# A two-layer decoder trunk on one core: each 128x128 weight block as three 256-column products instead of a 512-column and a 256-column one

## The chip, the cores and the metric

The kernel runs on one core of one Trainium2 chip. The metric is device time in microseconds (us) of one execution; lower is better. The engines are called as the profile calls them: PE (TensorE, the matrix unit; PEld are its weight loads), DVE (VectorE), ACT (ScalarE), POOL (GpSimd) and SP (SyncE, which issues the weight transfers).

## The reference, cut to what matters

```python
h = x                                   # (1, 256, 2048) f32
for i in range(2):
    hn = rmsnorm(h, norm_mix_pre[i])
    mix = ssd_mixer(hn, ...) if i == 0 else fox_mixer(hn, ...)   # Mamba-2 SSD / forgetting attention
    h = h + rmsnorm(mix, norm_mix_post[i])
    g = rmsnorm(h, norm_ffn_pre[i])
    ff = (silu(g @ w_gate) * (g @ w_up)) @ w_down                # 2048 -> 5632 -> 2048
    h = h + rmsnorm(ff, norm_ffn_post[i])
    pe = rmsnorm(p[i] @ ple_w_proj[i], ple_norm[i])
    h = h + sigmoid(h @ ple_w_gate[i]) * pe
```

Everything is float32, and there are 256 tokens. Nearly all arithmetic is in the products with weight matrices: `ssd_w_in` (2048 x 10304), `ssd_w_out` (4096 x 2048), `fox_w_in` (2048 x 6160), `fox_w_out` (2048 x 2048), and for each layer gate, up, down, the small projection and its gate.

## The kernel before, in words

All activations lie transposed, channels on the 128 partitions and the 256 tokens along the free axis. Each operand of the `float32r` products is split in two: a high part `wh` and a remainder `wl` of the weights, and a high and a low half of each activation tile. One block is one 128x128 weight block times one activation tile, and it needs three terms: wh by high, wh by low, wl by high.

**Activation tiles.** `halves()` makes a tile of 576 columns and returns a view of two rows of 256 columns, the high half at column 0 and the low half at column 308 (`LOW_X`). `x[:, 0, :]` is the high half, `x[:, 1, :]` the low one. The tiles are called `x`, `xq`, `xb` or `a` by the pool that they come from.

**Weights.** The list `stages` holds, in order, all pieces of weights, each of up to 1024 columns (1 to 4 row blocks of 128). `emit_stage` issues for one piece the transfer (L191, on SP's queue, into one of six `raw` buffers), the cast to `wh` (L204, on ACT) and the remainder `wl = raw - wh` (L209, on DVE); there are four buffers each of `wh` and `wl`. There are 1020 such pieces.

**Units.** `unit(rhs, evac, ...)` takes the pieces of one matrix with 4 (sometimes 2, 5 or 6) output tiles. It takes one PSUM bank of 512 columns for each output tile (`acc`, six banks in rotation), and for each piece issues the products of each output tile and row block. There are three forms:
- `tok` (L260 to L262): tokens on the partitions, used for the V matrix of the attention layer, three products of 412 or 416 columns.
- `sep` (L266 to L268): three products of 256 columns, all into the first half of the bank. Only the last unit of each output matrix uses it (`sep=last` and the like).
- otherwise (L271 and L274): one product of 512 columns with `wh`, whose two halves go into the two halves of the bank, and one product of 256 columns with `wl`, added to the first half. All other units use it.

After the last piece, `evac(t, acc)` reads each output tile. In the 512-column form the bank's two halves have to be added: `gather` (L299 to L301) copies the second half to `tb` with ACT (L300) and adds it to the first half with DVE (L301) into the wanted tile. What follows is one more DVE multiplication or addition in many callers: by `rwide2` for the gates (`silu_a`, L614) and the z tiles (L1139, L1074), by the gate for the up matrix (L664), by `rwide` ahead of the convolution (L916), by `rq` or `rwide` for q and k (L1359, L1366), or added to `m` for the second half of the down matrix (L680). In `out_units`, in the first half of the down matrix, for `gz` and in the first gate unit of each layer the gathered tile is stored as it is.

**Order.** The instruction order on each engine is made by a scheduler that simulates a timeline, within constraints: `after(...)` and `tc.issue_after` tie an instruction behind another on its engine, `bg` is a list of small background tasks, one of which is issued after each piece, and `low`, `turn`, `turn_a`, `low_a` and `lag` keep the last cast and remainder, and what has to stand ahead of the next ones. `took` hands `gather`'s two instructions to `unit`, which in units of six tiles puts them ahead of the next cast and remainder.

Of the kernel before, what the change touches and what calls it, by code (L numbers as in the profile page):

```python
# [14 lines left out]
P = 128  # L15
# [48 lines left out]
def tile_trunk(ctx, tc, a, out):  # L64
# [159 lines left out]
    def unit(rhs, evac, tok=False, pre=None, pops=1, late=(), merge=1, look=LOOK, sep=False):  # L224
# [10 lines left out]
        while k0 < K:  # L235
# [12 lines left out]
            with after(p0):  # L248
                p = None
                for t in range(nt):  # L250
                    with after(p if ordered else None):
                        for wh, wl, kc, kb in held:
                            for c in range(kc):
                                k = kb + c
                                x = rhs(k)
                                st, sp = k == 0, k == K - 1
                                if tok:
                                    xh = x[:, 0, t * P:(t + 1) * P]
                                    o = accs[t][:, :n]
                                    PE.matmul(o, lhsT=xh, rhs=wh[:, c, :], start=st, stop=False)  # L260
                                    PE.matmul(o, lhsT=xh, rhs=wl[:, c, :], start=False, stop=False)  # L261
                                    last = PE.matmul(o, lhsT=x[:, 1, t * P:(t + 1) * P], rhs=wh[:, c, :],  # L262
                                              start=False, stop=sp)
                                elif sep:
                                    o, w = accs[t][:, :T], wh[:, c, t * P:(t + 1) * P]
                                    PE.matmul(o, lhsT=w, rhs=x[:, 0, :], start=st, stop=False)  # L266
                                    PE.matmul(o, lhsT=w, rhs=x[:, 1, :], start=False, stop=False)  # L267
                                    last = PE.matmul(o, lhsT=wl[:, c, t * P:(t + 1) * P], rhs=x[:, 0, :],  # L268
                                              start=False, stop=sp)
                                else:  # L270
                                    PE.matmul(accs[t].rearrange("p (a n) -> p a n", a=2),  # L271
                                              lhsT=wh[:, c, t * P:(t + 1) * P], rhs=x,
                                              start=st, stop=False)
                                    last = PE.matmul(accs[t][:, :T], lhsT=wl[:, c, t * P:(t + 1) * P],  # L274
                                              rhs=x[:, 0, :], start=False, stop=sp)
                    p = last
# [21 lines left out]
    def gather(acc, o, np_=P):  # L298
        tb = tmp("tb")  # L299
        i = A.copy(out=tb[:np_], in_=acc[:np_, T:2 * T])  # L300
        took[0] = (i, V.tensor_tensor(out=o, in0=acc[:np_, :T], in1=tb[:np_], op=add))  # L301
# [281 lines left out]
    def out_units(sizes, rhs, m_of, pre=None):  # L583
        c0 = 0
        for u, n in enumerate(sizes):
            last = u == len(sizes) - 1

            def e(t, acc, c0=c0, last=last):
# [5 lines left out]
                else:  # L594
                    gather(acc, m[c])
                    sumsq(ssb, m[c], c == 0)
            unit(rhs, e, pre=pre if u == 0 else None, merge=TAIL_STAGES if last else 1,
                 sep=last)
            c0 += n

    def tail(i, mpx, m, pp, mk_next):
# [3 lines left out]
        with ExitStack() as st:  # L605
# [7 lines left out]
            def silu_a(sg):  # L613
                last_v[0] = V.tensor_tensor(out=sg, in0=sg, in1=rwide2, op=mult)  # L614
                th = tmp("th")
                mark[0] = A.activation(th, sg, AF.Tanh)
                return th
# [5 lines left out]
            def ev_g(t, acc):  # L623
                sg = new_sg()
                gather(acc, sg)
                sgs.append(sg)
                if not first[0]:
                    silu_b(sg, silu_a(sg))
# [15 lines left out]
            for half in range(2):  # L644
                acts = [halves(ap_, tag="a", name=nm("a")) for _ in range(HALF)]
                c0 = 0
                for n in (GU if half == 0 else GU[::-1]):
# [8 lines left out]
                    def ev_u(t, acc, c0=c0, acts=acts, begun=begun):  # L656
# [6 lines left out]
                        gather(acc, up)  # L663
                        V.tensor_tensor(out=up, in0=up, in1=sgs[t], op=mult)  # L664
# [4 lines left out]
                for u in range(4):  # L669
                    def e2(t, acc, u=u, half=half):  # L670
# [6 lines left out]
                        else:  # L677
                            t2 = tmp("g0")
                            gather(acc, t2)
                            V.tensor_tensor(out=m[c], in0=m[c], in1=t2, op=add)  # L680
                            sumsq(ssb, m[c], c == 0)
                    unit(lambda k, acts=acts: acts[k], e2,
                         merge=TAIL_STAGES if half == 1 and u == 3 else 1,
                         sep=half == 1 and u == 3)
# [110 lines left out]
        for u, (n, todo) in enumerate(zip(OUT0, (pops0, pops1, pops2, pops3))):  # L795
            last = u == len(OUT0) - 1
            up = None
            if u == 0:
# [6 lines left out]
                 merge=TAIL_STAGES if last else 1, sep=last)  # L805
# [22 lines left out]
    with ExitStack() as ys:  # L828
        yp = pool(ys, "yp", side="right")
        y = [yp.tile([P, T], F32, name=f"y{c}") for c in range(32)]  # L830
        with ExitStack() as st:
# [240 lines left out]
            def z_a(t):  # L1072
                z = later[t][0]
                last_v[0] = V.tensor_tensor(out=z, in0=z, in1=rwide2, op=mult)  # L1074
                zt[t] = tmp("th")
                lag[1].append(A.activation(zt[t], z, AF.Tanh))
# [39 lines left out]
            def z_unit(g, pops):  # L1116
                S = {}

                def ev_z(t, acc):
# [3 lines left out]
                    if t == 0:  # L1123
                        S["ss"] = ssp
                        if g == 0:
                            gated(0, z00)
# [7 lines left out]
                    gather(acc, z)  # L1134
                    gated(t, z)

                def gated(t, z):
                    yc = y[4 * g + t]
                    V.tensor_tensor(out=z, in0=z, in1=rwide2, op=mult)  # L1139
# [29 lines left out]
        for t in range(4):  # L1169
            acc, yc, ss = later[t]  # L1170
            z = zp.tile([P, T], F32, name=f"z7_{t}")
            gather(acc, z)
            later[t] = (z, yc, ss)
        turn_a[0] = took[0][0]
# [177 lines left out]
    for u in range(4):  # L1352
# [3 lines left out]
        def ev_q(t, acc, q=q):  # L1356
            g0 = tmp("g0")
            gather(acc, g0)
            V.tensor_tensor(out=q[t], in0=g0, in1=rq, op=mult)  # L1359
# [3 lines left out]
        def ev_k(t, acc, kk=kk):  # L1363
            g0 = tmp("g0")
            gather(acc, g0)
            V.tensor_tensor(out=kk[t], in0=g0, in1=rwide, op=mult)  # L1366
# [92 lines left out]
```

## Time and profile before

| | |
|---|---|
| time, median of 3 runs | 2738.63 us (2738.59 to 2739.45) |
| time of the profiled execution | 2740.92 us |
| its span in the profile | 2739.1 us |
| PE busy | 2730.2 us (100%), 16342 products |
| PEld busy | 2419.8 us (88%) |
| DVE busy | 1905.3 us (70%) |
| ACT busy | 1481.6 us (54%) |
| HBM read | 514.58 MB, 189 GB/s over the span |

A row of the groups reads: line of the program, engine, operation, output<-inputs, shape, count, busy time, mean duration of one, idle time before them and what ended it. Products overlap in PE's pipeline, so the duration of one is longer than the distance from its start to the next start; the pace of PE is read from the starts, in the rows in order of time or in the first and last start of a group.

### The profile page before, as it was taken

To read this page: it belongs to the slowest core of one execution; us is meant where nothing else is said; L and a number is where in the kernel's file an instruction comes from. 1 tells how busy PE (TensorE), PEld (TensorE's weight loads), DVE (VectorE), ACT (ScalarE), POOL (GpSimd) and SP (SyncE) were. 2 spreads that over 40 slices of the span, in tenths; PEclk is the share of its full clock that TensorE was granted. 3 is DMA by queue.
4 is the path that set the end of the run, shared out by engine and by line. 5 is a ranking of instruction groups with operands and counts; after the bars stand their busy time and mean duration, and the time that the engine had idled before them with its cause. 6 is when DMAs were issued, how large, how long until landed. Compare 5 with 4: busy or idle time off the path is not lost.

```text
span 2739.1 us, 43140 instructions
## 1 busy us (share of the span) xinstructions
PE 2730.2 (100%) x16342; PEld 2419.8 (88%) x16342; DVE 1905.3 (70%) x3147; ACT 1481.6 (54%) x2455; POOL 50.4 (2%) x108
## 2 busy tenths in 40 slices
PE   9999999999999999999999999999999999999999
PEld 8888888889888888888898998889888888888898
DVE  8888888755976645666668656766876546666577
ACT  6577677554654444445456544555654444445454
POOL 0000000000000000000000000000000000000000
PEclk9999999999999999999999999999999999999999
DMA  7666666565666556666556676655666556656555
GB/s 263 184 202 191 189 197 189 162 210 169 191 202 190 191 191 188 191 176 201 194 166 197 186 222 180 180 162 164 196 208 188 187 194 186 192 171 203 201 164 168
DMA packets 262688, 519.58 MB, mean 190 GB/s; under 512 B 17440, under 2 KB 44224, under 8 KB 262480
## 3 DMA queue, kind: packets, MB, share of 16 engines
q1 hardware_dynamic: 258784, 504.54, 60.0%
q0 software_dynamic: 3552, 12.15, 1.4%
q8 instruction: 128, 2.10, 0.3%
q14 instruction: 80, 0.66, 0.1%
q10 hardware_dynamic: 144, 0.14, 0.0%
HBM read 514.58 MB, written 2.18 MB: 189 GB/s over the span
## 4 chain that ended last, share of the span: by engine, by line
PE 96%; DVE 2%; ACT 1%; issue 1%; DMA 0%; ACTq 0%; DVEq 0%
PE acc L271 56%; PE acc L274 29%; PE acc L267 1%; PE acc L266 1%; PE acc L268 1%; PE acc L261 1%; PE acc L260 1%; PE acc L262 1%; PE mi L1025 1%; DVE wl L209 1%; ACT E L1005 0%; ACT wh L204 0%; PE mi L1289 0%; PE mi L1337 0%; DMA ab<-acd 0%
## 5 line engine op out<-in xcount | busy, mean ns | idle before, releaser
L271 PE MATMUL acc<-x,wh 128*128 128x512 f32 x4992 | 1687.9, 393 | 1.7 <-DVE gz L301 0.8
L209 DVE TENSOR_TENSOR wl<-raw,wh 128x1024 fp32r<-128x1024 f32 (+4 forms) x1020 | 1169.2, 1152 | 720.0 <-ACT wh L204 714.9
L204 ACT CAST wh<-raw 128x1024 fp32r<-128x1024 f32 (+4 forms) x1020 | 1006.4, 993 | 959.1 <-PE acc L271 834.1
L274 PE MATMUL acc<-x,wl 128*128 128x256 f32 x4992 | 1312.1, 279 | 1.0 <-DVE wl L209 0.7
L271 PEld LDWEIGHTS acc<-x,wh 128*128 128x128 f32 x4992 | 922.2, 188 | 187.8 <-DVE gz L301 1.5
L274 PEld LDWEIGHTS acc<-x,wl 128*128 128x128 f32 x4992 | 923.3, 188 | 27.5 <-DVE wl L209 3.9
L271 PE MATMUL acc<-a,wh 128*128 128x512 f32 x1232 | 424.7, 392 | 0.0
L274 PE MATMUL acc<-a,wl 128*128 128x256 f32 x1232 | 339.3, 280 | 0.0
L271 PEld LDWEIGHTS acc<-a,wh 128*128 128x128 f32 x1232 | 229.9, 188 | 48.9
L274 PEld LDWEIGHTS acc<-a,wl 128*128 128x128 f32 x1232 | 231.3, 188 | 2.2
L271 PE MATMUL acc<-xb,wh 128*128 128x512 f32 x512 | 177.6, 393 | 0.0
L300 ACT COPY tb<-acc 128x256 f32<-128x256 f32 x400 | 140.6, 370 | 47.6 <-PE acc L274 22.1
L274 PE MATMUL acc<-xb,wl 128*128 128x256 f32 x512 | 142.8, 280 | 0.0
L271 PEld LDWEIGHTS acc<-xb,wh 128*128 128x128 f32 x512 | 95.7, 188 | 19.7
L274 PEld LDWEIGHTS acc<-xb,wl 128*128 128x128 f32 x512 | 96.2, 188 | 0.9 <-issue 0.2
L271 PE MATMUL acc<-xq,wh 128*128 128x512 f32 x224 | 77.7, 392 | 0.0
L921 DVE SCALAR_TENSOR_TENSOR g<-xr,vec,g 128x256 f32<-128x256 f32 x144 | 63.3, 477 | 12.1 <-ACT g L918 11.9
L301 DVE TENSOR_TENSOR g<-acc,tb 128x256 f32<-128x256 f32 x171 | 65.1, 416 | 0.4
L274 PE MATMUL acc<-xq,wl 128*128 128x256 f32 x224 | 62.6, 280 | 0.0
L1005 ACT ACTIVATE E<-ab,bias 128x128 f32<-128x128 f32 x192 | 59.9, 392 | 3.0 <-DMA ab<-acd 3.0
L360 POOL TENSOR_TENSOR rs<-ms,mhalf 128x2 f32<-128x2 f32 x18 | 23.5, 1303 | 1984.3 <-DVE ms L357 1984.3
L324 DVE TENSOR_TENSOR ssb<-ssb,sq 128x256 f32<-128x256 f32 x120 | 50.4, 420 | 11.6 <-ACT sq L323 7.8
(230 smaller groups left out, 2154.0 us busy)
## 6 DMA issues: line engine op xcount, KB each, us to landing
raw<-down SPq DMA_DIRECT2D x176, 512.0 KB, 4.1
raw<-ssd_in SPq DMA_DIRECT2D x144, 512.0 KB, 4.5
raw<-gate SPq DMA_DIRECT2D x128, 512.0 KB, 4.3
raw<-up SPq DMA_DIRECT2D x128, 512.0 KB, 4.5
raw<-fox_in SPq DMA_DIRECT2D x64, 512.0 KB, 4.0
raw<-gate SPq DMA_DIRECT2D x64, 384.0 KB, 3.3
raw<-up SPq DMA_DIRECT2D x64, 384.0 KB, 3.5
raw<-ssd_out SPq DMA_DIRECT2D x40, 512.0 KB, 4.2
```

The costliest lines, as they stand in the source:

```text
L204: low_a[0] = A.copy(out=wh[:, :kc * n], in_=raw[:, :kc * n])
L209: low[0] = V.tensor_tensor(out=wl[:, :kc * n], in0=raw[:, :kc * n], in1=wh.bitcast(F32)[:, :kc * n], op=sub)
L260: PE.matmul(o, lhsT=xh, rhs=wh[:, c, :], start=st, stop=False)
L261: PE.matmul(o, lhsT=xh, rhs=wl[:, c, :], start=False, stop=False)
L262: last = PE.matmul(o, lhsT=x[:, 1, t * P:(t + 1) * P], rhs=wh[:, c, :], start=False, stop=sp)
L271: PE.matmul(accs[t].rearrange("p (a n) -> p a n", a=2), lhsT=wh[:, c, t * P:(t + 1) * P], rhs=x, start=st, stop=False)
L274: last = PE.matmul(accs[t][:, :T], lhsT=wl[:, c, t * P:(t + 1) * P], rhs=x[:, 0, :], start=False, stop=sp)
L300: i = A.copy(out=tb[:np_], in_=acc[:np_, T:2 * T])
L301: took[0] = (i, V.tensor_tensor(out=o, in0=acc[:np_, :T], in1=tb[:np_], op=add))
L324: last_v[0] = V.tensor_tensor(out=acc, in0=acc, in1=sq, op=add)
L921: V.scalar_tensor_tensor(out=c, in0=xr[:, k:k + T], scalar=col(f"conv_w{k}", cc), in1=c, op0=mult, op1=add)
L1005: A.activation(E[:, i, b * P:(b + 1) * P], ab[:, i, lo:lo + P], AF.Relu, scale=-1.0, bias=bias3[:, b, h0 + i:h0 + i + 1])
```

## The change

The `sep` form becomes the only one beside `tok`: every block is three products of 256 columns into the first half of its bank, and the parameter `sep` goes. `gather` is now one ACT copy out of PSUM. Where the caller multiplied or added right behind it, the new `gather_with` is one DVE instruction that reads PSUM and does that. So the copies to `tb` and the sums of the two halves go.

```diff
-                                elif sep:
+                                else:
                                     o, w = accs[t][:, :T], wh[:, c, t * P:(t + 1) * P]
                                     PE.matmul(o, lhsT=w, rhs=x[:, 0, :], start=st, stop=False)
                                     PE.matmul(o, lhsT=w, rhs=x[:, 1, :], start=False, stop=False)
                                     last = PE.matmul(o, lhsT=wl[:, c, t * P:(t + 1) * P], rhs=x[:, 0, :],
                                               start=False, stop=sp)
-                                else:
-                                    PE.matmul(accs[t].rearrange("p (a n) -> p a n", a=2),
-                                              lhsT=wh[:, c, t * P:(t + 1) * P], rhs=x,
-                                              start=st, stop=False)
-                                    last = PE.matmul(accs[t][:, :T], lhsT=wl[:, c, t * P:(t + 1) * P],
-                                              rhs=x[:, 0, :], start=False, stop=sp)
...
-    def gather(acc, o, np_=P):
-        tb = tmp("tb")
-        i = A.copy(out=tb[:np_], in_=acc[:np_, T:2 * T])
-        took[0] = (i, V.tensor_tensor(out=o, in0=acc[:np_, :T], in1=tb[:np_], op=add))
+    def gather(acc, o):
+        took[0] = (A.copy(out=o, in_=acc[:, :T]), None)
+
+    def gather_with(acc, o, other, op=mult):
+        took[0] = (None, V.tensor_tensor(out=o, in0=acc[:, :T], in1=other, op=op))
...
                         up = tmp("g0")
-                        gather(acc, up)
-                        V.tensor_tensor(out=up, in0=up, in1=sgs[t], op=mult)
+                        gather_with(acc, up, sgs[t])
                         split(up, acts[c0 + t])
...
-                gather(acc, xr[:, 3:])
-                V.tensor_tensor(out=xr[:, 3:], in0=xr[:, 3:], in1=rwide, op=mult)
+                gather_with(acc, xr[:, 3:], rwide)
...
         for t in range(4):
             acc, yc, ss = later[t]
             z = zp.tile([P, T], F32, name=f"z7_{t}")
-            gather(acc, z)
+            gather_with(acc, z, rwide2)
             later[t] = (z, yc, ss)
-        turn_a[0] = took[0][0]
         turn.append(took[0][1])
         low[0] = took[0][1]
```

The gates, the z tiles, q, k and the second half of the down matrix are changed in the same way. In the changed program L266 to L268 are the three products, L293 is the copy of `gather`, and L296 the instruction of `gather_with`.

How the instructions stand is shown at three places. The first is PE at the start of the first down unit of layer 0 (`a` are the 22 activation tiles of the hidden half; a piece holds two row blocks of four output tiles). Before:

```order
L271 MATMUL acc_10349<-a_7772,wh_10279 128x512
L274 MATMUL acc_10349<-a_7772,wl_10280 128x256
L271 MATMUL acc_10349<-a_7773,wh_10279 128x512
L274 MATMUL acc_10349<-a_7773,wl_10280 128x256
L271 MATMUL acc_10350<-a_7772,wh_10279 128x512
L274 MATMUL acc_10350<-a_7772,wl_10280 128x256
```

And in the changed kernel:

```order
L266 MATMUL acc_12388<-a_9233,wh_12314 128x256
L267 MATMUL acc_12388<-a_9233,wh_12314 128x256
L268 MATMUL acc_12388<-a_9233,wl_12315 128x256
L266 MATMUL acc_12388<-a_9234,wh_12314 128x256
L267 MATMUL acc_12388<-a_9234,wh_12314 128x256
L268 MATMUL acc_12388<-a_9234,wl_12315 128x256
L266 MATMUL acc_12389<-a_9233,wh_12314 128x256
L267 MATMUL acc_12389<-a_9233,wh_12314 128x256
L268 MATMUL acc_12389<-a_9233,wl_12315 128x256
```

The blocks stand in the same order, and each has three products, and so three weight loads, where it had two.

The second place is DVE at the end of an up unit of layer 0's first half, where the four accumulators are multiplied by the gates `sg` and split into the tiles `a`. Before:

```order
L209 TENSOR_TENSOR wl_9530<-raw_9527,wh_9529 128x1024
L306 TENSOR_TENSOR a_7782<-g_877_9473,a_7782 128x256
L306 TENSOR_TENSOR a_7783<-g_879_9480,a_7783 128x256
L301 TENSOR_TENSOR g_881_9487<-acc_9295,tb_9488 128x256
L301 TENSOR_TENSOR g_883_9494<-acc_9296,tb_9495 128x256
L664 TENSOR_TENSOR g_881_9487<-g_881_9487,sg_9275 128x256
L664 TENSOR_TENSOR g_883_9494<-g_883_9494,sg_9284 128x256
L306 TENSOR_TENSOR a_7784<-g_881_9487,a_7784 128x256
L306 TENSOR_TENSOR a_7785<-g_883_9494,a_7785 128x256
L209 TENSOR_TENSOR wl_9552<-raw_9549,wh_9551 128x1024
```

In the changed kernel (L301 is there the line of the split, L306 before):

```order
L296 TENSOR_TENSOR g_759_11316<-acc_11072,sg_11048 128x256
L209 TENSOR_TENSOR wl_11339<-raw_11336,wh_11338 128x1024
L296 TENSOR_TENSOR g_760_11320<-acc_11073,sg_11054 128x256
L301 TENSOR_TENSOR a_9243<-g_759_11316,a_9243 128x256
L296 TENSOR_TENSOR g_761_11324<-acc_11074,sg_11060 128x256
L209 TENSOR_TENSOR wl_11369<-raw_11366,wh_11368 128x1024
L301 TENSOR_TENSOR a_9244<-g_760_11320,a_9244 128x256
L301 TENSOR_TENSOR a_9245<-g_761_11324,a_9245 128x256
L296 TENSOR_TENSOR g_762_11328<-acc_11075,sg_11066 128x256
L209 TENSOR_TENSOR wl_11399<-raw_11396,wh_11398 128x1024
L301 TENSOR_TENSOR a_9246<-g_762_11328,a_9246 128x256
```

Each accumulator takes one DVE instruction less, and the remainders `wl` of the following pieces now stand between them.

The third place is ACT after the first unit of the last gate matrix (six tiles, layer 1), where the accumulators are copied to `gz`. Before, DVE added the halves there behind two remainders:

```order
L209 TENSOR_TENSOR wl_27756<-raw_27753,wh_27755 128x1024
L209 TENSOR_TENSOR wl_27762<-raw_27759,wh_27761 128x1024
L324 TENSOR_TENSOR ssp<-ssp,sq_27789 128x256
L301 TENSOR_TENSOR gz_27801<-acc_27406,tb_27802 128x256
L301 TENSOR_TENSOR gz_27805<-acc_27407,tb_27806 128x256
L324 TENSOR_TENSOR ssp<-ssp,sq_27792 128x256
```

Now ACT alone copies them:

```order
L204 CAST wh_33448<-raw_33446 128x1024
L204 CAST wh_33454<-raw_33452 128x1024
L293 COPY gz_33506<-acc_33015 128x256
L293 COPY gz_33508<-acc_33016 128x256
L204 CAST wh_33524<-raw_33522 128x1024
L293 COPY gz_33510<-acc_33017 128x256
```

The release of the banks no longer stands behind DVE's remainders there, only behind ACT's casts. Over the whole program DVE has 400 instructions less and ACT 299 less (400 copies to `tb` go, 101 copies of `gather` come), PE has 6960 products more, and SP's transfers stand in the same order.

More of the change, by code (lines that the diff above doesn't have):

```diff
@@ L222, in drain, with unit @@
             bg.popleft()()
-    def unit(rhs, evac, tok=False, pre=None, pops=1, late=(), merge=1, look=LOOK, sep=False):
+    def unit(rhs, evac, tok=False, pre=None, pops=1, late=(), merge=1, look=LOOK):
         K, cols, _ = plan[unit_i[0]]
@@ L596, in e @@
                     sumsq(ssb, m[c], c == 0)
-            unit(rhs, e, pre=pre if u == 0 else None, merge=TAIL_STAGES if last else 1,
-                 sep=last)
+            unit(rhs, e, pre=pre if u == 0 else None, merge=TAIL_STAGES if last else 1)
             c0 += n
@@ L611, in tail, with silu_a @@
             first = [True]
-            def silu_a(sg):
-                last_v[0] = V.tensor_tensor(out=sg, in0=sg, in1=rwide2, op=mult)
+            def silu_a(sg, acc=None):
+                if acc is None:
+                    last_v[0] = V.tensor_tensor(out=sg, in0=sg, in1=rwide2, op=mult)
+                else:
+                    gather_with(acc, sg, rwide2)
                 th = tmp("th")
@@ L624, in ev_g @@
                 sg = new_sg()
-                gather(acc, sg)
                 sgs.append(sg)
-                if not first[0]:
-                    silu_b(sg, silu_a(sg))
+                if first[0]:
+                    gather(acc, sg)
+                else:
+                    silu_b(sg, silu_a(sg, acc))
             def late_norm():
@@ L677, in e2 @@
                         else:
-                            t2 = tmp("g0")
-                            gather(acc, t2)
-                            V.tensor_tensor(out=m[c], in0=m[c], in1=t2, op=add)
+                            gather_with(acc, m[c], m[c], add)
                             sumsq(ssb, m[c], c == 0)
                     unit(lambda k, acts=acts: acts[k], e2,
-                         merge=TAIL_STAGES if half == 1 and u == 3 else 1,
-                         sep=half == 1 and u == 3)
+                         merge=TAIL_STAGES if half == 1 and u == 3 else 1)
         xs2 = [newx() for _ in range(NCH)]
@@ L804, in tail @@
                  pre=up, look=LOOK if u else 0,
-                 merge=TAIL_STAGES if last else 1, sep=last)
+                 merge=TAIL_STAGES if last else 1)
             c0 += n
@@ L1356, in ev_q @@
         def ev_q(t, acc, q=q):
-            g0 = tmp("g0")
-            gather(acc, g0)
-            V.tensor_tensor(out=q[t], in0=g0, in1=rq, op=mult)
+            gather_with(acc, q[t], rq)
         unit(lambda k: nxt[k], ev_q)
@@ L1363, in ev_k @@
         def ev_k(t, acc, kk=kk):
-            g0 = tmp("g0")
-            gather(acc, g0)
-            V.tensor_tensor(out=kk[t], in0=g0, in1=rwide, op=mult)
+            gather_with(acc, kk[t], rwide)
         unit(lambda k: nxt[k], ev_k)
```

13 lines of the change are left out of this document (5 added, 8 removed).

## The prediction

> **What bounds the kernel now.** I read the page first, then who waits for whom on PE and its weight loads, then PE's starts in order of time, because a busy PE says nothing of its pace.
>
> ```profile
> span 2739.1 us, 43140 instructions
> PE 2730.2 (100%) x16342; PEld 2419.8 (88%) x16342; DVE 1905.3 (70%) x3147; ACT 1481.6 (54%) x2455; POOL 50.4 (2%) x108
> PEclk9999999999999999999999999999999999999999
> PE 96%; DVE 2%; ACT 1%; issue 1%; DMA 0%; ACTq 0%; DVEq 0%
> ```
>
> PE is never without a product for long, at a full granted clock, and 96% of the chain that ended last is PE. The waits of PE and PEld are small; the largest that the change touches:
>
> ```profile
> PEld acc L274 <- DVE wl L209: 3.9, 10, 0.9
> PEld acc L271 <- DVE gz L301: 1.5, 2, 1.1
> PE acc L271 <- DVE gz L301: 0.8, 1, 0.8
> ```
>
> So the time is the number of products times PE's pace, and the question is what a block costs in each form. Both forms stand in this trace. The number of blocks in the two-product form is the sum of these counts, 4992 + 1232 + 512 + 224 = 6960:
>
> ```profile
> L271 PE MATMUL acc<-x,wh 128*128 128x512 f32 x4992 | 1687.9, 393 | 1.7 <-DVE gz L301 0.8 <-DVE x L413 0.7
> L271 PE MATMUL acc<-a,wh 128*128 128x512 f32 x1232 | 424.7, 392 | 0.0
> L271 PE MATMUL acc<-xb,wh 128*128 128x512 f32 x512 | 177.6, 393 | 0.0
> L271 PE MATMUL acc<-xq,wh 128*128 128x512 f32 x224 | 77.7, 392 | 0.0
> ```
>
> The pace of the two-product form, first in layer 0's down matrix (first half: 352 blocks in a row, the row of the tile's group gives the count, the rows in order of time the start and the first product after them):
>
> ```profile
> L271 PE MATMUL acc<-a,wh x352: 389/392/398, 930.7 to 1052.3; 128*128 128x512 f32 x176
> 930.68 0.39 PE L271 MATMUL acc<-a,wh 128*128 128x512 f32 x1
> 1052.65 0.39 PE L271 MATMUL acc<-x,wh 128*128 128x512 f32 x1
> ```
>
> (1052.65 - 930.68) / 352 = 346.5 ns a block. But the same two products also run faster in places, as in layer 1's last gate matrix, 9 blocks apart:
>
> ```profile
> 2673.51 0.39 PE L271 MATMUL acc<-x,wh 128*128 128x512 f32 x1
> 2676.57 0.39 PE L271 MATMUL acc<-x,wh 128*128 128x512 f32 x1
> ```
>
> 3.06 / 9 = 340.0 ns. So the form has two paces, and the mean needs long stretches. These three windows hold nothing but two-product blocks (busy time and count of L271's products and loads; a window's first product is the tail of the one ahead of it, so I take one off each count):
>
> ```profile
> 534.48:656.52 122.04, 121.82 (x353) 65.74 (x352) 1.00 0.64 207
> 751.30:1387.54 636.24, 628.22 (x1839) 341.96 (x1838) 1.00 0.62 192
> 1971.60:2608.01 636.41, 628.38 (x1840) 342.07 (x1839) 1.00 0.62 192
> ```
>
> 1394.69 us / 4029 blocks = 346.2 ns, small waits included. Now the three-product form, in the last down unit of the same layer, 88 blocks:
>
> ```profile
> L266 PE MATMUL acc<-a,wh x88: 276/276/286, 1387.6 to 1417.2; 128*128 128x256 f32 x88
> 1387.55 0.28 PE L266 MATMUL acc<-a,wh 128*128 128x256 f32 x1
> 1417.52 0.28 PE L457 MATMUL acc<-psp,wh 128*128 128x256 f32 x1
> ```
>
> (1417.52 - 1387.55) / 88 = 340.6 ns: three starts 113.5 ns apart. The same unit of layer 1 and the end of the first output matrix agree, from their first and last starts (29.6 / 87 = 340 ns, 10.6 / 31 = 342 ns, each within the last digit's 3 ns):
>
> ```profile
> L266 PE MATMUL acc<-a,wh x88: 276/276/286, 2608.0 to 2637.6; 128*128 128x256 f32 x88
> L266 PE MATMUL acc<-x,wh x32: 276/276/281, 656.5 to 667.1; 128*128 128x256 f32 x32
> ```
>
> **Step 1: the products.** 6960 blocks change form. For the 4029 of the windows the difference is 346.2 - 340.6 = 5.6 ns, 22.6 us. The other 2931 stand in the SSD mixer, the heads and middles of the tails and the attention, between other products, where a window can't be divided by one count; there I bound the old pace by 340.0 and 346.7 ns (the slow pace with its last digit) and both occur. That is -1.8 to +17.9 us of gain; I take the middle of the two paces plus a little, 344.5 ns, since the slow one holds in most of the windows: 3.9 ns x 2931 = 11.4 us. Step 1 gives **-34.0 us**, between -20.8 and -40.5.
>
> TensorE's weight loads rise from two to three a block. What covers them is the product running beside them, and the windows show how far (PE, PEld, DVE, ACT; clock, DMA share and GB/s at the end):
>
> ```profile
> 930.70:1052.60 121.90, 121.90 (x706) 107.24 (x705) 61.96 (x69) 52.44 (x64) 0.00 (x0) 1.00 0.59 190
> 1387.60:1417.50 29.90, 29.90 (x265) 29.90 (x265) 18.00 (x27) 13.58 (x19) 0.00 (x0) 1.00 0.54 169
> 200.00:300.00 100.00, 100.00 (x624) 87.02 (x623) 87.75 (x160) 69.68 (x136) 4.46 (x14) 1.00 0.63 194
> ```
>
> In the three-product stretch PEld is busy all the time (88% before it), so loads have no slack left, but their cost is already in the 113.5 ns, over 30 us and with DVE and ACT at work. The granted clock stays 1.00.
>
> A rule speaks against the change. The Trainium skill, "TensorE: Matmul & The Clock Gate", section "Back-to-back issue gap", gives an isolated product N/2.4 + 2.5 ns, so every product more costs a fixed 2.5 ns: by it 6960 x 2.5 = 17 us would be lost. The trace has the 512-column product 230 ns ahead of the next start, not the rule's 216, so its own measured pace decides against the rule here.
>
> **Step 2: the instruction program.** If the first queue carries PE's program, its bytes over twice 16342 instructions are 64 bytes each, and 13920 instructions more are 0.9 MB:
>
> ```profile
> q8 instruction: 128, 2.10, 0.3%
> ```
>
> In the 30 us stretch of 88 blocks 528 instructions, 34 KB, were fetched beside the products and no start came late. Cost 0 while that holds; 30 us is the longest that the trace shows of that rate.
>
> **Step 3: reading the accumulators.** The rows of the instructions that go or stay:
>
> ```profile
> L209 DVE TENSOR_TENSOR wl<-raw,wh 128x1024 fp32r<-128x1024 f32 (+4 forms) x1020 | 1169.2, 1152 | 720.0 <-ACT wh L204 714.9
> L301 DVE TENSOR_TENSOR g<-acc,tb 128x256 f32<-128x256 f32 x171 | 65.1, 416 | 0.4
> L300 ACT COPY tb<-acc 128x256 f32<-128x256 f32 x400 | 140.6, 370 | 47.6 <-PE acc L274 22.1
> L664 DVE TENSOR_TENSOR g<-g,sg 128x256 f32<-128x256 f32 x88 | 33.5, 416 | 0.1
> ```
>
> DVE loses 400 sums of 416 ns, 166 us; ACT loses 299 copies of 370 ns, 111 us. The 299 multiplications that remain (like L664) now read PSUM; L301 reads PSUM and L664 does not, and both take 416 ns, so their size stays. Neither engine is on the path: DVE is idle 30%, ACT 46%. What PE gets of it is the waits quoted at the top. A bank was free after a copy and a sum (370 + 416 ns in a row, with the sum behind remainders of 1152 ns); now after one of them. The 1.5 us for `gz` should mostly go, and half of the 3.9 us for `wl`: **-3 us**, bounded by 0 and -8 (all waits that name DVE). The other way, a new wait: L296 stands at the head of DVE until PE finishes its tile, with the next remainders queued behind it and PE waiting for those; but L301 waited for the same product through L300, so I count nothing, with an end of +5 us (a 1152 ns remainder late at four or five of the unit ends).
>
> **Step 4: what else is nearer.** Each piece has about 1.5% less time. ACT's casts, DVE's remainders and the DMA (share 0.54 to 0.64 in the windows) have room even in the SSD stretch, where DVE is at 88% and loses most per unit. Cost 0. The start, the V products of 412 columns and the tail after the last product don't change.
>
> **Sum.** 2740.9 for the profiled execution (2739.1 span and 1.8 around it) - 34.0 - 3 = 2703.9. The median of the runs shown is 2.3 us lower than the profiled one, 2738.6, so about **2702 us** by the median.
>
> **Rivals.**
>
> (a) *The three-product form has a slow pace too* (the slower side). The trace shows three-product runs with 412 columns, nine products apart:
>
> ```profile
> 1514.28 0.35 PE L260 MATMUL acc<-wh,xb 128*128 128x412 f32 x1
> 1515.97 0.35 PE L260 MATMUL acc<-wh,xb 128*128 128x412 f32 x1
> ```
>
> 1.69 / 9 = 187.8 ns, where 113.5 x 412/256 is 182.7: 2.8% slower. If long three-product stretches settle there, a block takes 350.1 ns, 4.2 more than the mean of the old form (345.5, step 1's two groups together), and 6960 of them are +29 us: 2768. It decides from 345.5 ns on, about half of that slow-down. Against it: the three quoted stretches, of 88, 88 and 32 blocks, ran at 340 to 342 ns over their whole length. The rule of the skill above, a fixed cost per product, would end on this side as well, at 2738.6 + 17 = 2756 by its figure; I put it with this case. Together 0.07.
>
> (b) *The old form runs fast in more of the kernel than I think, or part of the gain returns as waits.* If the 2931 blocks outside the windows are all fast now, step 1 gives -20.8 and step 3's +5 applies: 2723. For it: the fast pace does occur. Against it: 96% PE in the chain and few waits. 0.14 for 2712 to 2733.
>
> (c) *No change:* within 0.2% of before, 5.5 us, about what a measurement here can tell. It would take a return of 30 us in waits where now under 20 us are lost in all. 0.03.
>
> (d) *More than forecast:* all old blocks outside the windows slow (-40.5) and all DVE waits gone (-8): 2690. 0.06 below 2693.
>
> **Chances.** The forecast, 2693 to 2712, has 0.70. Faster by over 0.2%: 0.70 + 0.14 + 0.06 = 0.90; same 0.03; slower 0.07. The range is 2690 to 2720, which leaves out most of (a) and (c) and the upper part of (b), in all under 0.2.
>
> **What would show it.** Starts of L266, L267, L268 near 113.5 ns apart everywhere, 340.6 ns a block; PEld near 100% of the span; DVE near 1740 us and ACT near 1370 us busy; no wait for `gz`. Wrong if blocks take 345 ns or more in long stretches, or if PEld or PE waits for L296 or L209 add up to tens of us.

## The result and the profile after

The changed kernel takes 2704.57 us (median, 2704.28 to 2705.24) and the kernel before, run beside it, 2738.82 us (2738.59 to 2739.45): 34.3 us less, a ratio of 0.9875 with a 95% interval of 0.9858 to 0.9892. The profiled execution took 2704.73 us.

The page of the changed kernel, its span, busy times and granted clock:

```profile
span 2702.9 us, 56196 instructions
PE 2696.0 (100%) x23302; PEld 2680.0 (99%) x23302; DVE 1782.5 (66%) x2747; ACT 1398.9 (52%) x2156; POOL 46.8 (2%) x108
PEclk9999999999999999999999999999999999999999
```

PEld is now busy as long as PE (99%, 88% before). The pace, in the stretch that the prediction measured first (layer 0's down matrix, first half), from the group of the first product:

```profile
L266 PE MATMUL acc<-a,wh x352: 276/276/286, 918.3 to 1037.6; 128*128 128x256 f32 x176
```

(1037.6 - 918.3) / 351 = 339.9 ns a block, 346.5 before. The whole stretch of the gate, up and down matrices (busy time and count of PE, PEld, DVE, ACT, POOL; clock, DMA share, GB/s):

```profile
751.30:1387.54 636.24, 636.24 (x5610) 636.24 (x5609) 363.51 (x463) 285.08 (x350) 0.00 (x0) 1.00 0.65 194
```

5610 products in 636.24 us are 340.2 ns for three. PE's and PEld's waits that the change touches:

```profile
PE acc L266 <- DVE qk L296: 1.1, 2, 0.7
PEld acc L266 <- DVE qk L296: 1.5, 2, 0.9
```

The lists have no wait for `gz` or `wl` any more; two short ones for the readings of q and k are new.

From the starts of all products in the two traces: with the longer gaps between products (waits) set aside, a block took 345.5 ns before (6960 blocks) and 341.2 ns now (7296), and the gaps set aside fell by about 5 us. 6960 x 4.3 ns = 30 us and 5 us come near the 36.2 us between the two spans. So some five sixths of the gain are the pace of the products.

### The profile page after: what moved, and what is told of

Its sections match the earlier page's. It is cut to its first block, busy times and chain, and to the rows that moved or that the text cites. A ratio compares the mean times of both kernels' runs of the same rounds, so it can differ in the third digit from the quotient of the medians.

```text
span 2702.9 us, 56196 instructions
## 1 busy us (share of the span) xinstructions
PE 2696.0 (100%) x23302; PEld 2680.0 (99%) x23302; DVE 1782.5 (66%) x2747; ACT 1398.9 (52%) x2156; POOL 46.8 (2%) x108
## 3 DMA queue, kind: packets, MB, share of 16 engines
q8 instruction: 182, 2.98, 0.5%
## 5 line engine op out<-in xcount | busy, mean ns | idle before, releaser
L267 PE MATMUL acc<-x,wh 128*128 128x256 f32 x5120 | 1392.0, 277 | 0.0
L268 PE MATMUL acc<-x,wl 128*128 128x256 f32 x5120 | 1365.4, 276 | 0.0
L266 PE MATMUL acc<-x,wh 128*128 128x256 f32 x5120 | 1356.6, 277 | 0.1
L267 PEld LDWEIGHTS acc<-x,wh 128*128 128x128 f32 x5120 | 961.0, 188 | 2.0 <-issue 1.9
L268 PEld LDWEIGHTS acc<-x,wl 128*128 128x128 f32 x5120 | 948.2, 188 | 0.8 <-issue 0.7
L266 PEld LDWEIGHTS acc<-x,wh 128*128 128x128 f32 x5120 | 936.2, 188 | 1.4 <-issue 0.9
L267 PE MATMUL acc<-a,wh 128*128 128x256 f32 x1408 | 388.1, 276 | 0.0
L266 PE MATMUL acc<-a,wh 128*128 128x256 f32 x1408 | 388.0, 276 | 0.0
L268 PE MATMUL acc<-a,wl 128*128 128x256 f32 x1408 | 385.4, 275 | 0.0
L267 PEld LDWEIGHTS acc<-a,wh 128*128 128x128 f32 x1408 | 264.4, 188 | 0.0
L266 PEld LDWEIGHTS acc<-a,wh 128*128 128x128 f32 x1408 | 264.2, 188 | 0.0
L268 PEld LDWEIGHTS acc<-a,wl 128*128 128x128 f32 x1408 | 263.5, 188 | 0.0
L266 PE MATMUL acc<-xb,wh 128*128 128x256 f32 x512 | 143.8, 281 | 1.1 <-DVE qk L296 1.1
L267 PE MATMUL acc<-xb,wh 128*128 128x256 f32 x512 | 141.4, 276 | 0.0
L268 PE MATMUL acc<-xb,wl 128*128 128x256 f32 x512 | 140.6, 276 | 0.0
L266 PEld LDWEIGHTS acc<-xb,wh 128*128 128x128 f32 x512 | 96.1, 188 | 1.7 <-DVE qk L296 1.5
L267 PEld LDWEIGHTS acc<-xb,wh 128*128 128x128 f32 x512 | 96.2, 188 | 0.2
L268 PEld LDWEIGHTS acc<-xb,wl 128*128 128x128 f32 x512 | 95.8, 188 | 0.2 <-issue 0.2
L266 PE MATMUL acc<-xq,wh 128*128 128x256 f32 x256 | 70.7, 276 | 0.0
```

## The experiments

**The products alone.** Before, with the block as three products; the low term goes into the bank's second half, and the reading stays.

```diff
-                                    PE.matmul(accs[t].rearrange("p (a n) -> p a n", a=2),
-                                              lhsT=wh[:, c, t * P:(t + 1) * P], rhs=x, ...)
+                                    if st: ...      # a tile's first block stays 512 + 256
+                                    else:
+                                        PE.matmul(accs[t][:, :T], lhsT=w, rhs=x[:, 0, :], start=False, stop=False)
+                                        PE.matmul(accs[t][:, T:], lhsT=w, rhs=x[:, 1, :], start=False, stop=False)
```

> The kernel before with its blocks as three products, but the low half of the activations still into the second half of the bank, and the accumulators still read by copy and sum as before. (The first block of each output tile stays two products, some 390 of 6960.) If the gain is the products' pace, as forecast: about 6570 blocks times 4.4 to 5 ns, 29 to 33 us less than before, 2706 to 2710 us, with starts near 113.5 ns apart. If the gain is the lighter reading of the accumulators: 2733 to 2739 us, as before.

Measured: 2709.44 us, ratio 0.9891 (0.9877 to 0.9904), 29.5 us less than before, as expected if the products make the gain. The three products in the down matrix:

```profile
L276 PE MATMUL acc<-a,wh x336: 276/276/276, 920.9 to 1039.9; 128*128 128x256 f32 x168
```

These are 336 of the stretch's 352 blocks (each output tile's first block has another line); over all blocks that follow one another directly, the median is 340 ns. PEld still waits for the readings, `gz` as before and `sg` longer than before (0.4 us there), but the wait for `wl` is not in the list any more, although the reading was left as it was:

```profile
PEld acc L273 <- DVE gz L305: 1.8, 2, 0.9
PEld acc L273 <- DVE sg L305: 1.5, 2, 0.8
```

**The reading alone.** The changed `gather` and `gather_with` on the two products of before; the second half of the bank is left out of the sums.

```diff
-        tb = tmp("tb")
-        i = A.copy(out=tb[:np_], in_=acc[:np_, T:2 * T])
-        took[0] = (i, V.tensor_tensor(out=o, in0=acc[:np_, :T], in1=tb[:np_], op=add))
+        took[0] = (A.copy(out=o, in_=acc[:, :T]), None)
```

> The changed kernel's reading (one copy, or one DVE instruction out of PSUM) on the two-product form of before; the second half of each bank is written but not read, so the product of the high weights with the low activations is left out of the result in those units. If the gain is the products' pace: only the waits go, 0 to 5 us less than before, 2734 to 2739 us. If the reading made the gain: 2705 to 2715 us.

Measured: 2734.97 us, ratio 0.9985 (0.9977 to 0.9994), 4.0 us less. Its page and the same stretch of the down matrix:

```profile
PE 2727.7 (100%) x16342; PEld 2420.3 (89%) x16342; DVE 1782.2 (65%) x2747; ACT 1397.3 (51%) x2156; POOL 46.8 (2%) x108
L271 PE MATMUL acc<-a,wh x352: 389/392/398, 926.0 to 1047.8; 128*128 128x512 f32 x176
```

DVE and ACT are as free as in the changed kernel, and a block still takes (1047.8 - 926.0) / 351 = 347.0 ns: freeing DVE and ACT does not change the pace there. -29.5 and -4.0 add to -33.5 of the 34.3 measured.

**Products by themselves.** Ahead of the changed kernel, runs of 64 to 96 equal products on tiles of their own, with nothing beside them.

```diff
+        for j in range(64):
+            PE.matmul(mb2, lhsT=W[j % 4], rhs=m2, start=True, stop=True)          # 512 in two rows
...
+        for j in range(96):
+            PE.matmul(mb[:, :T], lhsT=W[j % 4], rhs=mx[:, :T], start=True, stop=True)
...
+        for j in range(96):
+            PE.matmul(mb[:, :P], lhsT=W[j % 4], rhs=mx[:, :P], start=True, stop=True)
```

> The changed kernel with ten runs of products on idle operands put ahead of it, each run of one kind, 64 or 96 long: 512 columns in two rows of 256, 512 in one row, 256, 384, 412, 128 and 64 columns, then 512 (two rows) and 256 in turn, 512 (one row) and 256 in turn, and three of 256. If columns alone set the pace at 0.443 ns each: 227, 227, 113.5, 170, 182.5, 57, 28 ns, and 340 ns a block for all three mixtures, so that the slow pace of the old form comes from its surroundings. If a weight load is the floor of a product: 128 and 64 columns take as long as 256 or nearly (over 100 ns). If the mixture of 512 and 256 is itself slow: 345 to 347 ns a block there, 340 for three of 256.

The groups of the products of 256 and of 128 columns:

```profile
L435 PE MATMUL mi<-mx,mw x96: 277/283/283, 34.9 to 46.3; 128*128 128x256 f32 x96
L441 PE MATMUL mi<-mx,mw x96: 220/275/280, 69.5 to 80.0; 128*128 128x128 f32 x96
```

256 columns: 11.4 / 95 = 120 ns, not the 113.5 of the kernel. 128 columns: 10.5 / 95 = 111 ns, and some thirty products of 64 columns were 111 to 112 ns apart too (from 84 us on the granted clock was 0.50 inside that group, and the rest of it says nothing). So with a weight load for each, a product of 128 or 64 columns takes some 111 ns, which looks like the load's own time; going below 256 columns has next to nothing to give. The Trainium skill, "TensorE: Matmul & The Clock Gate", section "LDWEIGHTS (loading the stationary operand)", gives a load its columns over 1.2 in ns, an estimated 107 ns for 128 columns; the row is close to it.

None of the mixtures took the 340 ns that the columns alone would give: 512 in two rows and 256 in turn took 350 ns once the clock was back, 512 in one row and 256 353 ns, and three of 256, the form of the changed kernel, 353 ns, against 340 in the kernel. Why the same instruction is slower by itself became the question.

**The low half next to the high half, old form.** `LOW_X` is where an activation's low half starts.

```diff
-LOW_X = 308
+LOW_X = 256
```

> The kernel before with the low half right behind the high half (offset 256 columns instead of 308), so the 512 columns are one run of addresses. If the slow pace of the two-product form is made by the addresses of the two halves, its blocks go to 340 ns and the time to 2705 to 2712 us, or they get slower still; if it is made by the alternation of a long and a short product, the time stays within 0.2% of before, 2733 to 2744 us.

Measured: 2724.46 us, ratio 0.9946 (0.9931 to 0.9962), 14.5 us less than before. In the down matrix:

```profile
L271 PE MATMUL acc<-a,wh x352: 388/389/394, 925.3 to 1044.9; 128*128 128x512 f32 x176
```

340.7 ns: the old form runs at its fast pace there. Neither expectation has the time, which lies between the two. The address matters, but it does not set the pace alone: in the kernel before, the same form on the same buffers runs at both paces, each for stretches of tens of blocks. Against the 346.5 ns of the down matrix stands a unit of layer 0's second half, in the trace of before, with (1265.8 - 1245.7) / 59 = 340.7 ns:

```profile
L271 PE MATMUL acc<-x,wh x60: 388/389/398, 1245.7 to 1265.8; 128*128 128x512 f32 x60
```

Of the 5991 blocks of two products that have the next such block right behind them, 1692 took 342 ns or less before and 4340 here. The offset makes the fast pace more frequent; what picks the pace of a stretch was not found.

**The same, new form.** The changed kernel with `LOW_X = 256`.

> The changed kernel with the low half at offset 256 instead of 308, the same edit that made the old form 14.5 us faster. If the weight load is the floor of a 256-column product (111 ns for 128 columns in the run of paces, 113.3 to 113.5 ns for 256 in the kernel), the address of the moving operand has nothing left to give: 2701 to 2708 us, within 0.15% of the changed kernel. If the address acts on both forms alike: 2688 to 2694 us.

Measured: **2790.94 us**, ratio to before 1.0189 (1.0175 to 1.0203), 86 us more than the changed kernel. Both expectations missed. The same stretch, and starts inside it:

```profile
L266 PE MATMUL acc<-a,wh x352: 280/280/281, 946.2 to 1070.2; 128*128 128x256 f32 x176
```

```profile
1000.25 0.28 PE L266 MATMUL acc<-a,wh 128*128 128x256 f32 x1
1000.37 0.28 PE L267 MATMUL acc<-a,wh 128*128 128x256 f32 x1
1000.49 0.28 PE L268 MATMUL acc<-a,wl 128*128 128x256 f32 x1
1000.61 0.28 PE L266 MATMUL acc<-a,wh 128*128 128x256 f32 x1
```

(1070.2 - 946.2) / 351 = 353.3 ns: all three products are about 118 ns apart, though only the second reads the low half. The three-product form has a slow pace.

**V in narrower pieces.** The changed kernel with the V matrix as eight units of 258 columns.

```diff
-    VW = (412, 412, 412, 412, 416)
+    VW = (258,) * 8
```

> The changed kernel with the V matrix as eight units of 258 columns instead of five of 412 to 416. If a narrow product runs at 113.5 ns per 256 columns there too: 768 products of 114.4 ns, 87.9 us, for 480 of 188.7 ns, 90.6 us, so about 2.7 us less, 2701 to 2703 us. If the slower pace of those products belongs to their operands and not to their width (as 188.7 is 2.8% to 3% over the columns' share): 768 of 117.5 ns, 90.2 us, no change, 2704 to 2706 us. Three units more, with their readings and fewer whole pieces, can add up to 3 us in both.

Measured: 2704.77 us, ratio to before 0.9873 (0.986 to 0.9887): as the changed kernel. Its V products, now of 258 columns, are 120 ns apart on average, the slow pace; the width was not what made V's products slow.

**Offsets, banks, sums and weights by themselves.** 64 products of 256 columns each, from weights and activations of their own, in groups that change one thing: the moving operand's start by 8, 16, 32, 64, 128, 256 or 384 columns, other weights, a running sum or not, two banks in turn.

```diff
+        for j in range(NR):
+            PE.matmul(mb[:, :T], lhsT=W[0], rhs=mx[:, 32:32+T], start=j == 0, stop=j == NR - 1)
...
+        for j in range(NR):
+            PE.matmul((mb, mc)[j % 2][:, :T], lhsT=W[0], rhs=mx[:, :T], start=True, stop=True)
```

> The changed kernel with fourteen runs of 64 products of 256 columns ahead of it: four weights in turn, each product its own sum; the same as one running sum; one weight throughout; one weight with the moving operand shifted by 8, 16, 32, 64, 128, 256 and 384 columns; the second, third and fourth weight; and two banks in turn. If the places of weight and moving operand set the pace: 113 ns at some of them and 117 to 122 ns at others, with the bank and the sum without effect. If the bank or the start of a sum sets it: 113 ns in the running sums or with two banks, 120 ns where each product starts anew in one bank, whatever the shift.

All groups took 117.8 to 120 ns (the first one once it had settled). Bank, sum and weight made no difference; of the start only steps that are no multiple of 64 columns did (117.8 to 118.7), and steps of 64 repeated 120.0. None reached 113.3.

**The old form with 320.** `LOW_X = 320` in the kernel before, also a multiple of 64, but with a gap between the halves.

> The kernel before with the low half at offset 320 columns (308 before, 256 in the contiguous run). If two rows instead of one run of 512 columns is what slows the old form: no better than 308, 2735 to 2742 us. If it is the distance of the halves, counted in some power of two, 320 = 5 x 64 behaves like 256: 2720 to 2730 us.

Measured: 2724.33 us, ratio 0.9945 (0.9931 to 0.9959), the same as with 256 (2724.46), and 4422 of the 5991 blocks took 342 ns or less. Contiguity is not what helped. 256 and 320 are both multiples of 64 columns, and 308 is not; these two runs alone do not show that the remainder by 64 is what counts.

**Distances.** Now each group of 48 products has its moving operand at a distance d (columns, modulo 64) behind the weight that is loaded beside it, and then the kernel's own mixtures follow, with the distances that the kernels' addresses have.

```diff
+        for j in range(NR):
+            PE.matmul(mb[:, :T], lhsT=w0, rhs=mx[:, 48:48+T], start=j == 0, stop=j == NR - 1)
...
+        for j in range(NR):        # three products as at LOW_X = 308 (then 304 for LOW_X = 256)
+            PE.matmul(mb[:, :T], lhsT=w0, rhs=mx[:, 48:48 + T], start=True, stop=False)
+            PE.matmul(mb[:, :T], lhsT=w0, rhs=mx[:, 356:356 + T], start=False, stop=False)
+            PE.matmul(mb[:, :T], lhsT=w1, rhs=mx[:, 48:48 + T], start=False, stop=True)
```

> The changed kernel with runs of 48 products ahead of it. First one weight and 256 moving columns, the moving operand 4, 12, 20, 24, 36, 40, 44, 48, 52, 56 and 60 columns behind a multiple of 64 from the weight. Theory A, the distance (start of the moving operand less start of the weight that is loaded beside it, modulo 64 columns of 4 bytes) sets the pace: 113 ns at 48 and 52, the distances of the changed kernel, 117 to 120 ns at most others (0, 8, 16 and 32 measured 120, 118, 118 and 119). Theory B, it doesn't: 118 to 120 ns at all. Then four mixtures at the kernel's own distances: the old pair with the low half at 308 and at 256, and the three products at 308 and at 256. A: the three products take 340 ns a block at 308 and 353 ns at 256; the old pair 346 or 340 ns, with 256 not slower than 308. B: both threes alike.

The groups for d = 44, 48 and 52, then the first products of the three-product mixture at 308 and at 256:

```profile
L446 PE MATMUL mi<-mx,mw x48: 279/282/287, 40.0 to 45.6; 128*128 128x256 f32 x48
L448 PE MATMUL mi<-mx,mw x48: 275/276/284, 45.7 to 51.1; 128*128 128x256 f32 x48
L450 PE MATMUL mi<-mx,mw x48: 278/281/288, 51.2 to 56.8; 128*128 128x256 f32 x48
```

```profile
L462 PE MATMUL mi<-mx,mw x48: 276/276/277, 100.9 to 116.8; 128*128 128x256 f32 x48
L466 PE MATMUL mi<-mx,mw x48: 276/281/282, 117.2 to 133.8; 128*128 128x256 f32 x48
```

With the starts to the nanosecond, d = 48 took 113.7 ns (113.3 once settled), 44 and 52 took 119.2, and the others (12 to 60) 117.3 to 120; d = 4, the first group, began slowly and took 116.6 in its second half. That 52 would be fast was expected and missed: of the fifteen distances tried (with 0, 8, 16 and 32 above), 48 alone is fast. The mixture took 340.0 ns at 308 and 353.3 at 256, the paces of the two kernels. The old pair took 340 ns at both, so its slow pace in the kernel did not come back here.

In the built program, modulo 64 columns, the high halves start at 56, the low ones at 44, `wh` at 8 and `wl` at 60. Beside wh by high the same `wh` is loaded again, beside wh by low `wl`, beside wl by high the next `wh`: 56 - 8, 44 - 60 and 56 - 8 are all 48. With `LOW_X = 256` the second becomes 60. The places themselves differ among these pairs, and in this run they are others again (the weight at 56, the moving operand at 40), so it is the distance that the fast products share. That it counts modulo 64 and not 128 shows in the kernel: its `x` tiles lie 576 columns apart, nine times 64, and all run at 340 ns.

**The weights moved.** The changed kernel, with only the `wh` buffers 48 columns further up (a filler that stood behind them now stands ahead of them). The distances become 0, 48 and 0; the activations stay where they are.

```diff
-    gap_l = pool(ctx, "gap_l")
     whp = pool(ctx, "whp")
+    gap_l = pool(ctx, "gap_l")
```

> The changed kernel with only the buffers of wh moved by 48 columns (the 48-column gap between wh and wl put ahead of wh); wl, the activations and the instructions stay. The distances (moving operand less the weight loaded beside it, modulo 64 columns) go from 48, 48, 48 to 0, 48, 0. Theory A, the distance sets the pace: 120 + 113.3 + 120 = 353 ns a block, 7296 blocks times 12 ns, 86 to 90 us more than the changed kernel, 2788 to 2796 us. Theory B, only the distance of the two halves of the activations matters: no change, 2702 to 2708 us.

Measured: **2792.49 us**, ratio to before 1.0196 (1.0181 to 1.0211), 88 us more than the changed kernel. The stretch of the down matrix:

```profile
L266 PE MATMUL acc<-a,wh x352: 277/281/285, 947.6 to 1071.7; 128*128 128x256 f32 x176
```

353.6 ns a block, with PE's 23302 products in the same order and no other operand moved. It is the distance, not the place of the activations. The block's time came out as expected, but not its parts: the three products are 117.4, 118.3 and 117.6 ns apart, not 120, 113.3 and 120. Two wrong distances cost what one did with `LOW_X = 256`.

**V's weights moved.** The changed kernel with V's `wh` and `wl` shifted by 32 columns and row blocks 448 apart, which makes V's distances 48 instead of 16.

```diff
-            return t[:, :kc * n].rearrange("p (c n) -> p c n", n=n)
+            return t[:, vsh:vsh + kc * ns].rearrange("p (c n) -> p c n", n=ns)[:, :, :n]    # 32, 448
```

> The changed kernel with V's weights 32 columns further into their buffers and their row blocks 448 columns apart instead of 412 (416), so that the distance in V's products goes from 16 (and 44 in the second row block) to 48 modulo 64. Theory A: 480 products at 0.443 ns a column, 182.5 ns instead of 188.7, 3 us less than the changed kernel, 2700.5 to 2702.5 us. Theory B: no change, 2703.5 to 2705.5 us; casts and remainders of V's pieces are in two runs of columns, which no wait should show.

Measured: 2704.04 us, ratio to before 0.9873 (0.9857 to 0.989), no change. V's products, of the changed kernel (L260) and of this one (L268):

```profile
L260 PE MATMUL acc<-wh,xb x160: 346/352/437, 1492.6 to 1583.5; 128*128 128x412 f32 x128, 128*128 128x416 f32 x32
L268 PE MATMUL acc<-wh,xb x160: 347/351/432, 1493.1 to 1584.3; 128*128 128x412 f32 x128, 128*128 128x416 f32 x32
```

From the first to the last of these starts there are 477 products: (1583.5 - 1492.6) / 477 = 190.6 ns in the changed kernel and 191.2 ns after the shift, with the small waits; without them 189.0 and 189.6. Theory A forecast 182.5 here and missed. For V the distance explains nothing, and why its products take 189 ns stays open.

**Block order at the starts of the tails.** The tail is the part of the program behind each layer's mixer. In the changed kernel 582 of 7296 blocks do not have their three products in a row (several wh by high come first); at 690 us 18 products take 2.12 us there, 353 ns a block. Here every product is tied behind the one ahead of it in block order.

```diff
-                                    PE.matmul(o, lhsT=w, rhs=x[:, 0, :], start=st, stop=False)
+                                    with after(b):
+                                        m1 = PE.matmul(o, lhsT=w, rhs=x[:, 0, :], start=st, stop=False)
+                                    with after(m1): ...
```

> The changed kernel with its products tied to the order of the blocks (wh by high, wh by low, wl by high of one block, then the next block); in the changed kernel 582 of 7296 blocks, at the starts of the tails and of the program, are issued by terms instead, several wh by high of different accumulators in a row. Theory A (distances): in order of terms the three distances are 48, 36 and 60 columns, so those blocks run at about 350 ns; in block order all three are 48 and they run at 340.3 ns, 582 x 9.7 = 5.6 us less, less what PE now waits there for the remainders wl that the order by terms let it wait for later (1 to 4 us): 2699 to 2704 us, with 340 to 341 ns a block in the stretch from 690 to 735 us. Theory B (those stretches are slow for the work of the other engines beside them): the pace there stays at 345 to 353 ns, and the waits are added: 2705 to 2709 us.

Measured: 2709.19 us, ratio to before 0.9892 (0.9875 to 0.9908), 4.6 us more than the changed kernel: next to B's number, and half of B's reason. The order of the changed kernel at 690 us, then two rows of PE in this run (L269 is wh by low here), and DVE's rows of the changed kernel in the same stretch:

```profile
690.54 0.86 PE L266 MATMUL acc<-x,wh 128*128 128x256 f32 x6
691.24 0.30 PE L267 MATMUL acc<-x,wh 128*128 128x256 f32 x1
691.38 0.28 PE L268 MATMUL acc<-x,wl 128*128 128x256 f32 x1
691.50 0.28 PE L267 MATMUL acc<-x,wh 128*128 128x256 f32 x1
```

```profile
690.39 0.35 PE L269 MATMUL acc<-x,wh 128*128 128x256 f32 x1
...
692.50 0.35 PE L269 MATMUL acc<-x,wh 128*128 128x256 f32 x1
```

```profile
690.63 0.48 DVE L512 SCALAR_TENSOR_TENSOR x<-h,vec,x 128x256 fp32r<-128x256 f32 x1
691.03 0.48 DVE L497 SCALAR_TENSOR_TENSOR sg<-m,vec,rwide 128x256 f32<-128x256 f32 x1
691.54 0.43 DVE L501 TENSOR_TENSOR h<-h,sg 128x256 f32<-128x256 f32 x1
691.88 0.95 DVE L209 TENSOR_TENSOR wl<-raw,wh 128x768 fp32r<-128x768 f32 x1
692.75 0.48 DVE L512 SCALAR_TENSOR_TENSOR x<-h,vec,x 128x256 fp32r<-128x256 f32 x1
```

A's distances do not hold in this stretch: behind the six wh by high, the other two terms alternate, so by the addresses every product there is 48 behind the weight beside it, as in block order, and still many were 117 to 119 ns apart. (Where terms do stand in rows, the distances are 36 and 60 as A says, and the trace of the changed kernel has 117.2 and 118.6 ns for 213 and 92 such products.) In block order most products of the stretch are 113.3 ns apart, but once per activation tile one step is longer (the rows with 0.35 us), and 18 products still take 2.11 us. The reason is in DVE's rows: four instructions without a gap, three for an activation tile and one remainder `wl`, take 2.12 us (692.75 - 690.63), and 18 products use one tile. The first unit here goes at DVE's pace, so a faster PE gains nothing; in block order the same steps of 2.1 us stand in layer 1's tail, from 1890 to 1911 us. And the waits that the fixed order adds (PE now waits for `x` by name, longest 0.9 us) cost more: over the whole trace the pace fell to 340.6 ns, about 4 us less, and the gaps grew by about 9 us.

## Why the prediction was right, step by step

**Step 1, the products** (-34.0, -20.8 to -40.5): right in kind and nearly in size. The products alone, with some 400 blocks left in the old form, measured -29.5. The old pace came out as forecast (345.5 ns over all blocks). For the 2931 blocks outside the windows that leaves 344.6 ns; the 344.5 of the forecast was a choice between two bounds and not a reading, so this close a hit is partly luck. The mis-sized term is the new pace: 340.6 ns was used for all 6960 blocks, and the mean is 341.2. Of the difference, 0.6 x 6960 = 4 us, some 3 us lie in the blocks whose products do not stand in a row (346 ns for three on average), most of them at the starts of the tails and of the program; the three quoted stretches held none.

What the step did not know is why 113.5 ns held. It was read from 208 blocks of the same program and carried over as a property of the form. It is a property of the form at these addresses: the last units of before used the same buffers as all others, so the extrapolation was sound within this kernel. With one buffer or one offset moved, the same instructions take 2791 or 2792 us, more than before; the prediction had no term for that, and rested, without knowing it, on a layout that was already there.

**Step 2, the instruction fetch** (0): right. The first queue grew from 2.10 to 2.98 MB, the 0.9 MB forecast, and PE's and PEld's waits show nothing for it:

```profile
q8 instruction: 182, 2.98, 0.5%
```

**Step 3, the reading** (-3, 0 to -8): right in size; -4.0 by itself, the wait for `gz` gone. The wait for `wl` went with the reading alone, but also with the products alone, so it is not the reading's own gain. The new wait behind L296 exists, for q and k, at 1.5 us against the +5 us of its bound. The busy times were off: DVE fell by 123 us and not by 166, ACT by 83 and not by 111. A row's mean duration was multiplied by the count, while the durations of neighbours overlap: L301's own row had 65.1 us busy for 171, 381 ns each and not 416; 400 of those are 152 us. The rest of the difference was not followed, and the path does not hang on it.

**Step 4** (0): right over the long stretches; the first unit of the tail at 690 us, and by the steps of 2.1 us also that of layer 1, where DVE sets the pace, are an exception that the step did not see.

**Rival (a)**, the slow pace of the three-product form: it did not decide here, but it exists, with a larger price than was worked out (353.3 ns and +52 us against before, not 350.1 and +29). Its sum has a slip: 350.1 is 4.6 ns above 345.5 and not 4.2, which makes +32 us ahead of the 3 us of the waits. V's 187.8 ns, its evidence, did not follow the distance and is not explained. The rule that was put with it, a fixed cost for each product, is not what decides: moving an address, with the same products, makes 86 and 88 us. **Rival (b)**: the kernel before did have the fast pace in 1692 of the 5991 blocks counted above, but not in most; with `LOW_X` at 256 or 320 it comes in most of them, for 14.5 us.

Open: what picks between the old pair's two paces in the kernel, at the same addresses (by itself it ran at 340 ns with the same distances); why V's products do not follow the distance; why one wrong distance of three slows all three (113.3 + 117.3 + 113.3 = 343.9 by single prices, 353.3 measured) and two cost no more; and how the old form would do with the weights moved, which no run tried.

## What to carry to other kernels

A pace that was read from stretches of the same program, over 30 us with the other engines at work, forecast well here, where the operands stayed in the same buffers; before a pace is carried to other buffers, measure it there. Where products and weight loads both fill their time, vary the distance of their operands in the local memory before judging a form by its instructions: the place of a filler of 48 columns was worth 88 us here, more than twice the change itself. And where PE's pace is off in one stretch, look at the engine that makes its operands first: where DVE needs 2.12 us from one tile to the next, a better order does not use the tiles faster.

## What the runs showed of the hardware that was not expected

- A product of 256 columns takes 113.3 ns when its moving operand starts 48 columns (of 4 bytes, modulo 64) behind the weight that is loaded beside it, and 116.6 to 120 ns at the fourteen other distances tried. In blocks of three it is 340.0 against 353.3 ns. The Trainium skill, "TensorE: Matmul & The Clock Gate", section "Step-by-step: what each phase is for", says that loading the next weights takes no read bandwidth from the running product, since each has a port of its own. No run here measures that bandwidth; the time of a product beside a load does depend on where both lie.
- With a weight load for each, products of 64 and of 128 columns took 111 to 112 ns, those of 256 columns 113.3 at best.
- A pair of 512 and 256 columns took 340 or 346 to 347 ns on the same buffers of the kernel before, and kept either pace for tens of pairs.
- A product of 412 columns took 186.6 ns by itself (distance 0), and 189.0 and 189.6 in the kernel at distances of 16 and 44 and of 48.
